# The values' projection moved between the recurrent group's convolutions and its gates

## The chip, the cores and the metric

The kernel runs on one core of a Trainium2 chip. The metric is the device time of one execution in microseconds (us). The kernel before has a median of 602.1 us in three runs (601.52 to 603.06).

The engines are called PE (matrix products), ACT (activations, casts), DVE (elementwise work and scans), POOL, and SP (here the queue that issues most transfers). Each works through its own list of instructions in order and waits where an input or a buffer is not ready.

## The reference

One decoder layer: 512 positions, 1024 features, all in float32.

```python
h = rms_norm(x, g_pre_mix)
q, k, v, xr, gr = split(h @ w_in)              # 512 columns each
attn = moba_attention(q, k, v, rel_bias)       # 8 heads of 64
xr = causal_dwconv(xr, w_conv_lru, b_conv_lru) # 4 taps per channel
r, i = sigmoid(xr @ w_r + b_r), sigmoid(xr @ w_i + b_i)  # block-diagonal
a = exp(-8 * r * softplus(-lam))
u = sqrt(1 - a * a) * (i * xr)
lru = scan(h_t = a_t * h_{t-1} + u_t) * gelu(gr)
x = x + rms_norm(concat(attn, lru) @ w_out, g_post_mix)
# then a convolved gated FFN (w_up, w_conv_ffn, w_down) in the same manner
```

## The kernel before

Every product of two float32 matrices is made of three matmuls on a high and a low part of each operand (`mm3`, lines 79 to 81: high*high, high*low, low*high). The split of an operand is a cast on ACT (`split`, line 84: `wh`, `xsh`, `mixTh`) and a subtraction on DVE (line 85: `wl`, `xsl`, `mixTl`). A weight block is loaded into a tile `raw` or `rawqk` (two buffers), split into `wh` and `wl` (four buffers each), and multiplied with `hTh`, `hTl`, the transposed normalized input.

The mixing stage, up to about 105 us, goes in this order in the source:

- `px`: the recurrent group's input (column `xr`), four blocks `t` of 128 channels, each 24 matmuls of 512 columns (the first two blocks in halves of 256). ACT starts each convolution with `xc` (line 309) and DVE adds three taps (line 311).
- Gates of block `t`, in the same loop: `xc` is split into `xsh`, `xsl` (one buffer each), six matmuls make `pg0` and `pg1` (line 317), and ACT and DVE make `a`, `g` and `y` of them (lines 321 to 332). The sigmoids are written with Tanh; Exp, Tanh, Abs and Square are used.
- `pv`: the values, four PSUM banks of 24 matmuls each (lines 335 to 344), split into `vhl` (line 356).
- `pgr`: the column `gr`, four blocks of 24 matmuls, each followed by a Gelu on ACT (line 362). Ahead of these in the source stands one Sqrt over all four blocks of `gv` (line 358).
- The scan: per block two multiplications (lines 364, 366) and one scan (line 365) on DVE, and the split of the result into `mixTh`, `mixTl` (line 367).
- `pq`: queries and keys of the first pair of heads, then attention pair by pair: scores `psc`, a softmax on DVE and ACT, transposes `ptp`, products `pav`. While a pair is in work, the next pair's `pq` matmuls are put between its steps.

The source order is not the order on the engines. The framework's scheduler fixes each engine's list when the program is built: it takes matmuls of one group between those of another, and moves casts and subtractions forward and back. An activation table load is put in front of an ACT function whose table isn't the active one.

Of the kernel before, what the change touches and what calls it, by code (L numbers as in the profile page):

```python
# [18 lines left out]
P = 128  # L19
# [5 lines left out]
DA = H * DH  # L25
DL = 512
NT = S // P
KD = D // P
# [24 lines left out]
def hybrid_layer(  # L53
# [8 lines left out]
    w_in, w_out, w_up, w_down = w_in[0], w_out[0], w_up[0], w_down[0]  # L62
# [7 lines left out]
    def bank(name, tag):  # L70
        return ps.tile([P, 512], F32, tag=tag, name=name, bufs=BANKS[tag])
# [5 lines left out]
    def mm3(o, lhs, rhs, start, stop):  # L77
        (lh, ll), (rh, rl) = lhs, rhs
        nc.tensor.matmul(o, lh, rh, start=start, stop=False)  # L79
        nc.tensor.matmul(o, lh, rl, start=False, stop=False)  # L80
        nc.tensor.matmul(o, ll, rh, start=False, stop=stop)  # L81

    def split(h, l, src, sub=None):
        nc.scalar.copy(h, src)  # L84
        (sub or nc.vector).tensor_sub(l, src, f32(h))  # L85

    def load_raw(src, k, n):
        t = wp.tile([P, k, n], F32, tag="raw", name="raw", bufs=2)
        nc.sync.dma_start(t, src.rearrange("(k p) n -> p k n", p=P))
        return t  # L90

    def split_w(src, k, n, sub=None):
        h = wp.tile([P, k, n], F32R, tag="wh", name="wh")
        l = wp.tile([P, k, n], F32R, tag="wl", name="wl")
        split(h, l, src, sub)
        return h, l

    def at(hl, *idx):
        return hl[0][idx], hl[1][idx]
# [57 lines left out]
    hT = [cp.tile([P, KD, S], F32R, tag=f"hT{i}", name=f"hT{i}") for i in "hl"]  # L157
# [61 lines left out]
    def w_conv_l(tap, t):  # L219
        return par[:, 4 * tap + t:4 * tap + t + 1]  # L220

    def col(c):
        return par[:, c:c + 1]
# [49 lines left out]
    def kpos(t):  # L273
        return sp[:, 6, t:t + 1]

    def kneg(t):
        return sp[:, 7, t:t + 1]
# [4 lines left out]
    def project(w, pt, c0=0, c1=S):  # L282
        for k in range(KD):
            mm3(pt[:, c0:c1], at(w, slice(None), k), at(hT, slice(None), k, slice(c0, c1)),
                k == 0, k == KD - 1)


    xc = lp.tile([P, NT, S], F32, name="xc")
    av = lp.tile([P, NT, S], F32, name="av")
# [3 lines left out]
    def xr_block(t):  # L293
        return split_w(raw_xr[t // 2][:, :, (t % 2) * P:(t % 2 + 1) * P], KD, P), bank("px", "mm")
# [5 lines left out]
    for t in range(NT):  # L300
        if t < 2:
            px = first[t][1]
        else:
            if t == 2:
                raw_xr.append(load_raw(w_in[:, XR0 + 256:XR0 + 512], KD, 256))
            w, px = xr_block(t)
            project(w, px)
        c = xc[:, t]
        nc.scalar.activation(c, px, AF.Identity, scale=w_conv_l(3, t), bias=col(16 + t))
        for d in range(1, 4):  # L310
            nc.vector.scalar_tensor_tensor(
                c[:, d:], px[:, :S - d], w_conv_l(3 - d, t), c[:, d:], op0=ALU.mult, op1=ALU.add)
        xs = [lp.tile([P, S], F32R, tag=f"xs{i}", name=f"xs{i}") for i in "hl"]
        split(xs[0], xs[1], c)
        pg = [bank(f"pg{g}", "sc") for g in range(2)]
        for g in range(2):
            mm3(pg[g], at(gw, slice(None), g, t), (xs[0], xs[1]), True, True)


        a, g, y = av[:, t], gv[:, t], gl[:, t]  # L320
        nc.vector.tensor_scalar(a, pg[0], col(20 + t), 0.0, op0=ALU.add, op1=ALU.min)
        nc.scalar.activation(g, pg[0], AF.Abs, scale=0.5, bias=half_b[:, t:t + 1])
        nc.scalar.activation(y, pg[1], AF.Tanh, scale=0.5, bias=half_b[:, 4 + t:5 + t])
        nc.vector.scalar_tensor_tensor(c, y, 1.0, c, op0=ALU.add, op1=ALU.mult)
        nc.scalar.activation(a, a, AF.Exp)
        nc.scalar.activation(g, g, AF.Tanh)
        nc.vector.scalar_tensor_tensor(g, g, 1.0, a, op0=ALU.add, op1=ALU.mult)

        nc.scalar.activation(a, g, AF.Exp, scale=kneg(t))
        nc.scalar.activation(g, g, AF.Tanh, scale=kpos(t))  # L330
        nc.scalar.activation(y, a, AF.Square)
        nc.vector.scalar_tensor_tensor(g, y, 1.0, g, op0=ALU.add, op1=ALU.mult)


    pv = [bank(f"pv{t}", ("tr", "tr", "av", "mm")[t]) for t in range(NT)]
    for c in range(2):
        raw = load_raw(w_in[c * 512:(c + 1) * 512, 2 * DA:3 * DA], 4, DA)
        for u in range(2):
            w = split_w(raw[:, 2 * u:2 * u + 2], 2, DA)
            for j in range(2):  # L340
                k = 4 * c + 2 * u + j
                for t in range(NT):
                    mm3(pv[t], at(hT, slice(None), k, slice(t * P, (t + 1) * P)),
                        at(w, slice(None), j), k == 0, k == KD - 1)

    def gr_block(t):
        if t % 2 == 0:
# [246 lines left out]
    for i2 in range(NF // 2):  # L594
        raws = [load_raw(w_up[:, o + 256 * i2:o + 256 * (i2 + 1)], KD, 256) for o in (0, DFF)]
        blocks = [[], []]
        for b in range(2):
            for r in raws:
                w = split_w(r[:, :, b * P:(b + 1) * P], KD, P, None if i2 else nc.gpsimd)
# [55 lines left out]
```

## Time and profile before

| | |
|---|---|
| median of 3 runs | 602.1 us |
| the profiled execution's own time | 601.9 us |
| its span in the trace | 600.1 us |
| PE busy | 581.0 us (97% of the span), 2704 matmuls |
| DVE busy | 364.0 us (61%) |
| ACT busy | 277.6 us (46%) |
| granted PE clock, mean | 0.993 |

The span runs from the first to the last instruction of the profiled execution; 1.8 us of its time lie outside. Busy matmuls overlap, since one starts before the one ahead of it has ended: the pace is the distance of their starts, not their duration. A start-to-start distance is used for ACT and DVE as well where instructions follow each other without a wait.

### The profile page before, as it was taken

The page shows a single profiled execution, that of the slowest core. Times are in us where ns is not written, and L with a number is a line of the kernel's source. Part 1 is how long each engine was busy: PE and PEld are TensorE (multiplying, and loading weights), DVE is VectorE, ACT ScalarE, POOL GpSimd, SP SyncE. Part 2 cuts the span into 40 slices and gives each one's busy share as a digit, 9 for nine tenths or more (in the row PEclk, how much of TensorE's full clock was granted, in tenths as well). Part 3 has the DMA queues.
Part 4 walks back from the last instruction along what each step waited for, and adds up shares of the span by engine and source line. Part 5 has one row for each costly group of instructions (what it writes and reads, how often), then busy time and mean ns, then how long its engine had stood idle before and what let it go on. Part 6 is the DMA issues. An engine that isn't in the chain of part 4 may idle for free.

```text
span 600.1 us, 6975 instructions
## 1 busy us (share of the span) xinstructions
PE 581.0 (97%) x2704; PEld 475.9 (79%) x2704; DVE 364.0 (61%) x660; ACT 277.6 (46%) x455; POOL 11.6 (2%) x12
## 2 busy tenths in 40 slices
PE   6999999999999997999999999999999999999995
PEld 3977888677778876988888888888888888888884
DVE  5869694788885688476566566665665622232225
ACT  7539954667765463454344443443444412231221
POOL 1000000000000033000000000000000000000000
PEclk9999999999999998999999999999999999999998
DMA  7552445233020405044034124224314421332103
GB/s 229 188 211 72 139 117 163 72 106 97 9 71 1 140 2 175 1 141 141 13 128 140 52 90 141 70 71 140 97 44 141 134 77 37 140 114 97 35 1 140
DMA packets 52265, 59.62 MB, mean 99 GB/s; under 512 B 2448, under 2 KB 41568, under 8 KB 52233
## 3 DMA queue, kind: packets, MB, share of 16 engines
q1 hardware_dynamic: 51201, 57.61, 29.8%
q10 hardware_dynamic: 1032, 1.57, 0.8%
q8 instruction: 21, 0.34, 0.2%
q14 instruction: 11, 0.09, 0.0%
HBM read 57.06 MB, written 3.69 MB: 101 GB/s over the span
## 4 chain that ended last, share of the span: by engine, by line
PE 92%; DVE 4%; ACT 2%; DMA 1%; issue 0%; SPq 0%; DVEq 0%
PE pup L80 13%; PE pup L79 13%; PE pup L81 13%; PE py L79 9%; PE py L80 9%; PE py L81 9%; PE pq L79 3%; PE pq L80 2%; PE pq L81 2%; PE psc L425 2%; PE pav L451 2%; PE ptp L441 2%; PE px L81 1%; PE px L79 1%; PE px L80 1%; PE pv L79 1%
## 5 line engine op out<-in xcount | busy, mean ns | idle before, releaser
L85 DVE TENSOR_TENSOR wl<-raw,wh 128x1024 fp32r<-128x1024 f32 x82 | 100.2, 1222 | 133.9 <-ACT wh L84 133.2
L84 ACT CAST wh<-raw 128x1024 fp32r<-128x1024 f32 x86 | 89.9, 1048 | 156.0 <-PE py L81 72.0
L80 PE MATMUL pup<-h2Tl,wh 128*128 128x512 f32 (+1 forms) x384 | 143.4, 373 | 2.0 <-DVE h2Tl L85 2.0
L81 PE MATMUL pup<-h2Th,wl 128*128 128x512 f32 (+1 forms) x384 | 143.5, 374 | 0.0
L79 PE MATMUL pup<-h2Th,wh 128*128 128x512 f32 (+1 forms) x384 | 143.3, 373 | 0.0
L80 PEld LDWEIGHTS pup<-h2Tl,wh 128*128 128x128 f32 x384 | 73.1, 190 | 14.5 <-DVE h2Tl L85 2.3
L79 PEld LDWEIGHTS pup<-h2Th,wh 128*128 128x128 f32 x384 | 73.1, 190 | 12.6
L81 PEld LDWEIGHTS pup<-h2Th,wl 128*128 128x128 f32 x384 | 73.0, 190 | 12.5
L79 PE MATMUL py<-wh,acth 128*128 128x512 f32 x176 | 68.5, 389 | 0.0
L80 PE MATMUL py<-wl,acth 128*128 128x512 f32 x176 | 68.5, 389 | 0.0
L81 PE MATMUL py<-wh,actl 128*128 128x512 f32 x176 | 68.5, 389 | 0.0
L81 PEld LDWEIGHTS py<-wh,actl 128*128 128x128 f32 x176 | 33.0, 188 | 6.9
L80 PEld LDWEIGHTS py<-wl,acth 128*128 128x128 f32 x176 | 33.0, 188 | 6.8
L79 PEld LDWEIGHTS py<-wh,acth 128*128 128x128 f32 x176 | 33.0, 188 | 6.8
L589 ACT ACTIVATE yg<-yg 128x512 f32<-128x512 f32 x22 | 13.9, 633 | 42.7 <-DVE yg L582 42.7
L582 DVE SCALAR_TENSOR_TENSOR yu<-pup,par,yu 128x511 f32<-128x511 f32 (+1 forms) x44 | 33.0, 749 | 0.8
L582 DVE SCALAR_TENSOR_TENSOR yg<-pup,par,yg 128x511 f32<-128x511 f32 (+1 forms) x44 | 32.8, 746 | 0.8
L79 PE MATMUL pq<-hTh,wh 128*128 128x512 f32 x64 | 26.5, 414 | 0.0
L80 PE MATMUL py<-wl,mixTh 128*128 128x512 f32 x64 | 25.8, 404 | 0.0
L81 PE MATMUL py<-wh,mixTl 128*128 128x512 f32 x64 | 25.5, 399 | 0.0
L81 PE MATMUL pq<-hTh,wl 128*128 128x512 f32 x64 | 25.5, 399 | 0.0
L79 PE MATMUL py<-wh,mixTh 128*128 128x512 f32 x64 | 25.4, 397 | 0.0
(164 smaller groups left out, 849.0 us busy)
## 6 DMA issues: line engine op xcount, KB each, us to landing
raw<-in_w_up_dram SPq DMA_DIRECT2D x22, 1024.0 KB, 5.2
raw<-in_w_down_dram SPq DMA_DIRECT2D x10, 1024.0 KB, 5.0
raw<-in_w_in_dram SPq DMA_DIRECT2D x5, 1024.0 KB
rawqk<-in_w_in_dram SPq DMA_DIRECT2D x8, 512.0 KB, 5.2
raw<-in_w_out_dram SPq DMA_DIRECT2D x4, 1024.0 KB, 5.1
xres<-in_x_dram SPq DMA_DIRECT2D x4, 512.0 KB, 6.0
out_dram<-yz SPq DMA_DIRECT2D x8, 256.0 KB, 2.0
toep<-fbd ACTq DMA_DIRECT2D x1, 1536.0 KB
```

What stands on the lines that cost most here:

```text
L79: nc.tensor.matmul(o, lh, rh, start=start, stop=False)
L80: nc.tensor.matmul(o, lh, rl, start=False, stop=False)
L81: nc.tensor.matmul(o, ll, rh, start=False, stop=stop)
L84: nc.scalar.copy(h, src)
L85: (sub or nc.vector).tensor_sub(l, src, f32(h))
L425: nc.tensor.matmul(psc[:, :W], qs[own[s], s, qi], kl[own[s], :W], start=False, stop=True)
L441: nc.tensor.transpose(ptr[:, j * P:(j + 1) * P], st[:, j * P:(j + 1) * P], ident)
L451: nc.tensor.matmul(pav[:, j * P:], vs, pT[i][:, j * S:j * (S - P) + S], start=j == 0 and i == 0, stop=j == NT - 1 and i == 1)
L582: nc.vector.scalar_tensor_tensor(y[:, d:], pt[:, :S - d], w_conv_f(2 - d, blk), y[:, d:], op0=ALU.mult, op1=ALU.add)
L589: nc.scalar.activation(yg, yg, AF.Gelu_apprx_tanh)
```

## The change

The loop over `t` is cut in two. The first loop keeps the projections `px` and the convolutions. Then come the values (`pv`), and after them a second loop with the split of `xc`, the gate products and the gate functions. No instruction of the computation is added or taken away.

```diff
         for d in range(1, 4):
             nc.vector.scalar_tensor_tensor(
                 c[:, d:], px[:, :S - d], w_conv_l(3 - d, t), c[:, d:], op0=ALU.mult, op1=ALU.add)
-        xs = [lp.tile([P, S], F32R, tag=f"xs{i}", name=f"xs{i}") for i in "hl"]
-        split(xs[0], xs[1], c)
-        pg = [bank(f"pg{g}", "sc") for g in range(2)]
...
-        nc.vector.scalar_tensor_tensor(g, y, 1.0, g, op0=ALU.add, op1=ALU.mult)
     pv = [bank(f"pv{t}", ("tr", "tr", "av", "mm")[t]) for t in range(NT)]
...
                 for t in range(NT):
                     mm3(pv[t], at(hT, slice(None), k, slice(t * P, (t + 1) * P)),
                         at(w, slice(None), j), k == 0, k == KD - 1)
+
+
+    for t in range(NT):
+        c = xc[:, t]
+        xs = [lp.tile([P, S], F32R, tag=f"xs{i}", name=f"xs{i}") for i in "hl"]
+        split(xs[0], xs[1], c)
+        pg = [bank(f"pg{g}", "sc") for g in range(2)]
+        for g in range(2):
+            mm3(pg[g], at(gw, slice(None), g, t), (xs[0], xs[1]), True, True)
+
+
+        a, g, y = av[:, t], gv[:, t], gl[:, t]
+        nc.vector.tensor_scalar(a, pg[0], col(20 + t), 0.0, op0=ALU.add, op1=ALU.min)
+        nc.scalar.activation(g, pg[0], AF.Abs, scale=0.5, bias=half_b[:, t:t + 1])
+        nc.scalar.activation(y, pg[1], AF.Tanh, scale=0.5, bias=half_b[:, 4 + t:5 + t])
+        nc.vector.scalar_tensor_tensor(c, y, 1.0, c, op0=ALU.add, op1=ALU.mult)
+        nc.scalar.activation(a, a, AF.Exp)
+        nc.scalar.activation(g, g, AF.Tanh)
+        nc.vector.scalar_tensor_tensor(g, g, 1.0, a, op0=ALU.add, op1=ALU.mult)
+
+        nc.scalar.activation(a, g, AF.Exp, scale=kneg(t))
+        nc.scalar.activation(g, g, AF.Tanh, scale=kpos(t))
+        nc.scalar.activation(y, a, AF.Square)
+        nc.vector.scalar_tensor_tensor(g, y, 1.0, g, op0=ALU.add, op1=ALU.mult)
```

Lines from the gates on have other numbers in the change: the gate lines 321 to 332 become 337 to 348, the Sqrt 358 becomes 362, the Gelu 362 becomes 366, the scan lines 364 to 366 become 368 to 370, `vhl` 356 becomes 360. The lists of the two programs differ on the engines at three places that matter below. A number behind a name tells buffers apart; `wh_842` and `wh_846` belong to the first pair's queries and keys (`pq_850`, `pq_875`), `wl_920` to the second pair's queries (`pq_937`).

On PE, around 41 us of the trace before, where the fourth block of `px` begins (`px_506` before, `px_437` in the change). Before:

```order
L79 MATMUL pv1_559<-wh_592,hTh_82 128x512
L79 MATMUL pv2_560<-wh_592,hTh_82 128x512
L79 MATMUL px_506<-hTh_82,wh_502 128x512
L79 MATMUL pg0_398<-xsh_394,gwh_108 128x512
L79 MATMUL pg1_399<-xsh_394,gwh_108 128x512
L80 MATMUL px_506<-hTl_83,wh_502 128x512
```

In the change:

```order
L79 MATMUL pv1_467<-wh_500,hTh_82 128x512
L79 MATMUL pv2_468<-wh_500,hTh_82 128x512
L79 MATMUL px_437<-hTh_82,wh_433 128x512
L80 MATMUL px_437<-hTl_83,wh_433 128x512
L81 MATMUL px_437<-hTh_82,wl_434 128x512
```

The gate products of the first block no longer stand behind the first matmul of `px`. They now stand 99 matmuls later, behind the last matmul of `pv`; those of the blocks 1 to 3 follow 20, 41 and 76 matmuls behind the first ones, between the `pgr` matmuls.

On ACT, from the end of the gates to the first `pgr` Gelu. Before:

```order
L356 CAST vhl_93<-pv0_558 128x4x2x64
L358 ACT_TABLE_LOAD
L358 ACTIVATE gv_282<-gv_282 128x2048
L84 CAST wh_694<-raw_688 128x1024
L356 CAST vhl_93<-pv1_559 128x4x2x64
L356 CAST vhl_93<-pv2_560 128x4x2x64
L356 CAST vhl_93<-pv3_561 128x4x2x64
L84 CAST wh_842<-rawqk_839 128x1024
L362 ACT_TABLE_LOAD
L362 ACTIVATE gl_283<-pgr_707 128x512
```

In the change, the piece from the third Gelu to the fourth:

```order
L366 ACT_TABLE_LOAD
L366 ACTIVATE gl_283<-pgr_759 128x512
L345 ACT_TABLE_LOAD
L345 ACTIVATE av_281<-gv_282,sp_253 128x512
L84 CAST wh_842<-rawqk_839 128x1024
L346 ACTIVATE gv_282<-gv_282,sp_253 128x512
L347 ACTIVATE gl_283<-av_281 128x512
L84 CAST wh_846<-rawqk_839 128x1024
L362 ACT_TABLE_LOAD
L362 ACTIVATE gv_282<-gv_282 128x2048
L366 ACT_TABLE_LOAD
L366 ACTIVATE gl_283<-pgr_785 128x512
```

The first three Gelus stand among the gates of blocks 1 to 3, each with a table load ahead of it and another behind it. From the first gate function to the last Gelu ACT has eight table loads where it had two. The cast `wh_842`, which stood ahead of the first Gelu, now stands behind the third and behind the Exp of the last block, and the Sqrt stands behind `wh_846`.

On DVE, from the split of the keys' weights `wl_847` to the split of the second pair's weights. Before:

```order
L365 SCALAR_TENSOR_TENSOR gv_282<-av_281,xc_280 128x512 x2
L85 TENSOR_TENSOR mixTl_89<-gl_283,mixTh_88 128x512
L85 TENSOR_TENSOR wl_843<-rawqk_839,wh_842 128x1024
L85 TENSOR_TENSOR wl_847<-rawqk_839,wh_846 128x1024
L366 TENSOR_TENSOR gl_283<-gl_283,gv_282 128x512
L85 TENSOR_TENSOR mixTl_89<-gl_283,mixTh_88 128x512
L85 TENSOR_TENSOR wl_920<-rawqk_916,wh_919 128x1024
```

In the change:

```order
L85 TENSOR_TENSOR wl_847<-rawqk_839,wh_846 128x1024
L368 TENSOR_TENSOR xc_280<-xc_280,gv_282 128x512 x2
L369 SCALAR_TENSOR_TENSOR gv_282<-av_281,xc_280 128x512 x2
L370 TENSOR_TENSOR gl_283<-gl_283,gv_282 128x512 x2
L368 TENSOR_TENSOR xc_280<-xc_280,gv_282 128x512 x2
L85 TENSOR_TENSOR mixTl_89<-gl_283,mixTh_88 128x512 x2
L369 SCALAR_TENSOR_TENSOR gv_282<-av_281,xc_280 128x512 x2
L370 TENSOR_TENSOR gl_283<-gl_283,gv_282 128x512 x2
L85 TENSOR_TENSOR wl_920<-rawqk_916,wh_919 128x1024
```

All four scans (line 365, now 369) stood ahead of `wl_843` before; in the change they stand, with their multiplications, between `wl_847` and `wl_920`.

## Rows read from the trace of the kernel before

**Rows 1.** The page's part on the chain of work that ended last: shares of the span by engine.

```profile
PE 92%; DVE 4%; ACT 2%; DMA 1%; issue 0%; SPq 0%; DVEq 0%
```

**Rows 2.** PE's waits over the whole span: tile and line that waited, what it waited for, us in total, times, longest us.

```profile
PE ptr L151 <- DVE hn L145: 4.8, 3, 3.0
PE pup L80 <- DVE h2Tl L85: 2.0, 1, 2.0
PE pg L79 <- issue: 1.5, 1, 1.5
```

**Rows 3.** PE's timeline at the fourth `px` block: start us, duration us, engine, line, operation, in brackets the idle time before it.

```profile
41.05 0.39 PE L79 MATMUL px<-hTh,wh 128*128 128x512 f32 x1
42.90 0.70 PE L79 MATMUL pg<-xsh,gwh 128*128 128x512 f32 x2 [1.46 <-issue]
```

**Rows 4.** ACT's timeline at the same place.

```profile
41.23 1.04 ACT L84 CAST wh<-raw 128x1024 fp32r<-128x1024 f32 x1 [3.04 <-DMA raw<-in_w_in_dram]
42.19 0.61 ACT L84 CAST xsh<-xc 128x512 fp32r<-128x512 f32 x1
```

**Rows 5.** PE's timeline: the first `pgr` matmul, the first and the third of the first pair's `pq` (96 and 98 matmuls later), and the third of the second pair's (48 later again).

```profile
71.13 0.39 PE L79 MATMUL pgr<-hTh,wh 128*128 128x512 f32 x1
...
92.89 0.39 PE L79 MATMUL pq<-hTh,wh 128*128 128x512 f32 x1
...
93.34 0.39 PE L81 MATMUL pq<-hTh,wl 128*128 128x512 f32 x1
...
104.22 0.39 PE L81 MATMUL pq<-hTh,wl 128*128 128x512 f32 x1
```

**Rows 6.** ACT's timeline, a stretch of gate functions that follow each other without a wait.

```profile
48.91 0.69 ACT L323 ACTIVATE gl<-pg,half_b 128x512 f32<-128x512 f32 x1 [1.06 <-PE pg L81]
49.49 0.71 ACT L329 ACTIVATE av<-gv,sp 128x512 f32<-128x512 f32 x1
50.11 0.68 ACT L322 ACTIVATE gv<-pg,half_b 128x512 f32<-128x512 f32 x1
50.67 0.72 ACT L330 ACTIVATE gv<-gv,sp 128x512 f32<-128x512 f32 x1
51.29 0.62 ACT L331 ACTIVATE gl<-av 128x512 f32<-128x512 f32 x1
51.81 0.62 ACT L325 ACTIVATE av<-av 128x512 f32<-128x512 f32 x1
52.33 0.62 ACT L326 ACTIVATE gv<-gv 128x512 f32<-128x512 f32 x1
52.85 0.61 ACT L84 CAST xsh<-xc 128x512 fp32r<-128x512 f32 x1
53.36 0.79 ACT L309 ACTIVATE xc<-px,par 128x512 f32<-128x512 f32 x1
```

**Rows 7.** ACT's timeline: the Sqrt and the first Gelu with their table loads, and the cast `wh_842` between.

```profile
69.89 1.28 ACT L358 ACT_TABLE_LOAD   x1
71.19 1.92 ACT L358 ACTIVATE gv<-gv 128x2048 f32<-128x2048 f32 x1
...
76.54 1.05 ACT L84 CAST wh<-rawqk 128x1024 fp32r<-128x1024 f32 x1 [1.05 <-PE pgr L80]
77.62 1.28 ACT L362 ACT_TABLE_LOAD   x1
78.91 0.60 ACT L362 ACTIVATE gl<-pgr 128x512 f32<-128x512 f32 x1
```

**Rows 8.** DVE's timeline: two scans, two multiplications, one multiplication, and the splits `wl_843` and `wl_847`.

```profile
77.28 2.33 DVE L365 TENSOR_TENSOR_SCAN gv<-av,xc 128x512 f32<-128x512 f32 x2
79.53 1.27 DVE L364 TENSOR_TENSOR xc<-xc,gv 128x512 f32<-128x512 f32 x2
80.71 0.69 DVE L366 TENSOR_TENSOR gl<-gl,gv 128x512 f32<-128x512 f32 x1
...
84.15 2.36 DVE L85 TENSOR_TENSOR wl<-rawqk,wh 128x1024 fp32r<-128x1024 f32 x2
```

**Rows 9.** Stretches of the span: from:to, length, busy us (instructions) of PE, PEld, DVE, ACT, POOL, then the granted PE clock (1.00 is 2.4 GHz, 0.50 is 1.2 GHz), DMA share, GB/s.

```profile
42.00:43.00 1.00, 0.10 (x1) 0.13 (x2) 0.17 (x1) 0.80 (x2) 0.00 (x0) 1.00 0.43 159
...
226.00:227.00 1.00, 0.82 (x6) 0.82 (x7) 1.00 (x3) 0.00 (x0) 1.00 (x1) 0.91 0.00 0
227.00:228.00 1.00, 1.00 (x7) 1.00 (x7) 1.00 (x1) 0.00 (x0) 0.76 (x1) 0.50 0.00 0
...
230.00:231.00 1.00, 1.00 (x9) 1.00 (x9) 0.91 (x4) 1.00 (x4) 0.00 (x0) 0.88 1.09 388
...
235.00:236.00 1.00, 0.98 (x9) 1.00 (x10) 1.00 (x2) 0.32 (x1) 0.00 (x0) 1.00 0.85 241
...
595.50:596.00 0.50, 0.00 (x0) 0.00 (x0) 0.46 (x2) 0.00 (x0) 0.00 (x0) 0.50 0.00 0
```

**Rows 10.** PE's timeline: matmuls of 256 columns at either level of the clock.

```profile
227.56 0.41 PE L79 MATMUL pup<-h2Th,wh 128*128 128x256 f32 x1
227.78 0.41 PE L80 MATMUL pup<-h2Tl,wh 128*128 128x256 f32 x1
...
230.42 0.28 PE L81 MATMUL pup<-h2Th,wl 128*128 128x256 f32 x1
230.54 0.28 PE L79 MATMUL pup<-h2Th,wh 128*128 128x256 f32 x1
```

More of the change, by code (lines that the diff above doesn't have):

```diff
@@ L312, in hybrid_layer @@
                 c[:, d:], px[:, :S - d], w_conv_l(3 - d, t), c[:, d:], op0=ALU.mult, op1=ALU.add)
+    pv = [bank(f"pv{t}", ("tr", "tr", "av", "mm")[t]) for t in range(NT)]
+    for c in range(2):
+        raw = load_raw(w_in[c * 512:(c + 1) * 512, 2 * DA:3 * DA], 4, DA)
+        for u in range(2):
+            w = split_w(raw[:, 2 * u:2 * u + 2], 2, DA)
+            for j in range(2):
+                k = 4 * c + 2 * u + j
+                for t in range(NT):
+                    mm3(pv[t], at(hT, slice(None), k, slice(t * P, (t + 1) * P)),
+                        at(w, slice(None), j), k == 0, k == KD - 1)
+    for t in range(NT):
+        c = xc[:, t]
         xs = [lp.tile([P, S], F32R, tag=f"xs{i}", name=f"xs{i}") for i in "hl"]
@@ L332, in hybrid_layer @@
         nc.vector.scalar_tensor_tensor(g, y, 1.0, g, op0=ALU.add, op1=ALU.mult)
[L335 to L344, printed above, removed]
     def gr_block(t):
```

## The prediction

> **What bounds the kernel now.** I read the chain of work that ended last first: 92% of it is PE [rows 1]. So a change is worth what it adds to or takes from PE's waits, and the next view is the list of these. Up to the end of attention it has one wait at the place of the change: 1.5 us at `pg` [rows 2]. PE's timeline there shows the first `px` matmul of the fourth block at 41.05 and the next matmul, the first gate product, at 42.90 [rows 3]. ACT's timeline says why: the cast `xsh`, which the gate product reads, starts only at 42.19, behind a weight cast that waited 3.04 us for its load until 41.23 [rows 4]. That load is the second half of the values' weights, which PE doesn't need yet.
>
> From there PE runs without a listed wait into attention. Its pace is (92.89 - 71.13) / 96 = 0.2267 us per matmul of 512 columns [rows 5]. ACT and DVE have slack in this stretch, but they feed PE from short lists of buffers, so the question is when ACT and DVE reach the splits for `pq`.
>
> **What the change saves.** The first gate products leave their place behind `px`. PE goes on at 41.05 + 0.23 = 41.28 instead of 42.90: 1.62 us saved. What covers the late load now is the rest of `px` and the values' matmuls on the first half of their weights: 51 matmuls x 0.2267 = 11.6 us, up to 52.6, while the cast of the late half ends at 42.3. Without that cover the 1.62 us would come back. The number of matmuls is the same, so their work costs nothing more.
>
> **What it moves, first term: `pq` waits for its weights.** The gate functions now start after the values. The last `pv` matmul starts 98 places behind 41.05, at 63.3, and ends at 63.7. ACT has one weight cast ahead of the rest, whose buffer is only free then (1.04, by [rows 4]), and a cast of `vhl`, which I take like a gate cast at 0.52. The first Tanh starts near 65.2, when its product is also done. From here ACT's list is summed with the distances of starts in [rows 6]: Tanh of the gate 0.58, Abs 0.56, both Exp 0.52 and 0.62, the other Tanhs 0.52 and 0.62, Square 0.52, cast `xsh` 0.51 (0.61 where something waits for its end). A table load takes 1.30 up to the next function, a Gelu 0.60 [rows 7].
>
> - Block 0: 0.58 + 0.56 + 0.52 + 0.52 + 0.51 = 2.69, up to 67.9. Then a wait of 0.6 for DVE, which has a `wl`, a `vhl` and two gate pieces ahead of the one that is needed (1.13 and three to four at 0.6 by [rows 8], from 64.8). Then 0.72 + 0.62 + 0.52, up to 70.4.
> - Block 1: the five pieces to the end of `xsh` without Abs, 0.58 + 0.52 + 0.52 + 0.61, and Abs 0.56: 2.8. Load, Gelu, load: 3.2. Exp, the next block's Abs, Tanh, Square: 2.32. Up to 78.7.
> - Block 2: the same without the first Abs, 2.23 + 3.2 + 2.32, up to 86.5.
> - Block 3: 0.58 + 0.52 + 0.62, load, Gelu, load 3.2, Exp 0.62, up to 92.0; then `wh_842`, 1.05, up to 93.1.
>
> PE, with 219 matmuls behind 41.05 and some 0.6 us lost at the gate products (0.4 of it a wait for `xsl` of block 1, behind the same DVE pieces), would be at `pq` at 91.3. It waits for `wh_842` till 93.1, and for the third matmul, which reads `wl_843`, until 93.1 + 1.23 [rows 8] = 94.4. Before, that matmul started at 93.34 [rows 5]. So the saving is gone here and PE is 1.1 us late. In the kernel before the same cast ran at 76.54 [rows 7], 16 us ahead of its use: the cover is used up by six more table loads (7.8 us) and by gates that start 20 us later.
>
> The Trainium skill, page "ScalarE: Activation LUTs", section "What ACT_TABLE_LOAD costs", puts a switch at about 2.66 us: 1.28 for the load and 1.38 for a drain. The trace agrees with the first part (1.28) and shows no room for the second: the load at 77.62 follows a cast that ends at 77.59, and the Gelu starts 0.01 behind the load [rows 7]. By the page's figure as an estimate, six more switches would put another 6 x 1.38 = 8.3 us into ACT's sum and the whole near 618.
>
> **Second term: the second pair's weights wait behind the scan.** After `wh_842` ACT has Tanh, Square and `wh_846` (up to 95.2), a load (96.5) and the Sqrt, 1.92 [rows 7], up to 98.4. Only then can DVE start the first multiplication of the recurrence. Its list up to `wl_920` is five pairs at 1.2 (a pair starts 80.71 - 79.53 = 1.18 ahead of the next piece), two pairs of scans at 2.25, and the split itself at 1.23 [rows 8]: 6.0 + 4.5 + 1.2 = 11.7, up to 110.1, and 110.2 with the handovers. The Gelu of the last block (97.7) and the casts of `mixTh` on ACT lie beside this. PE would be at the third matmul of `pq_937`, which reads `wl_920`, 48 x 0.2267 = 10.9 us behind 94.4, at 105.3. It waits 4.9 us there. Nothing else is queued on PE that could go ahead: it takes its matmuls in order. Before, that matmul started at 104.22 [rows 5], so PE is now 6.0 us late. This includes the 1.62 saved and the 1.1 above; it is not added to them.
>
> **Third term: the clock.** A PE that sits idle for 4.9 us may lose its clock. Rows of both kinds exist. After the 1.96 us idle at `pup` (2.0 in [rows 2]) the granted clock was 0.91 in the microsecond from 226 and 0.50 in the next, and 0.88 in that from 230 [rows 9]: some 3.3 us at 1.2 GHz. After the 3.0 us at `ptr` it stayed at 1.00 in the microsecond from 235, as it did after the 1.5 us at 42 [rows 2, 9]. At the end of the program, where no matmul follows, it was 0.50 from 595.5. At the lower level 256 columns took 0.22 against 0.12 [rows 10]; 15 of them fit into 3.3 us, and 15 x 0.095 = 1.4 us is the price. Bounds: 0 and, for two such stretches, 2.8. I take 1.4, since this idle time is longer than any of the three above. A fall during the wait at `pq_850` costs nothing: PE waits for DVE behind it anyway.
>
> **Sum.** 601.9 (the profiled execution) + 6.0 + 1.4 = 609.3. The median of the runs is 0.2 above the profiled one, so 609.5. Nothing after `pq_937` is counted. DVE comes to the first softmax some 2.3 us later in relation to PE than before, which the slower matmuls just then would cover; if they don't, 1 to 2 us more are lost, and this goes into the range. The queue of SP keeps its order up to the bias tables `tb`, which now stand ahead of the last pair's weights; the tables wait for the last `mixTl`, near 111.6, and are read by the first softmax near 116, some 4 us, so I count no wait there.
>
> **Rivals.** (a) *The saving alone.* If ACT and DVE reach `wh_842` and `wl_920` in time after all, only the 1.62 us are left: 602.1 - 1.6 = 600.5. For it speaks the 16 us that `wh_842` had in hand before [rows 7]; against it the sums above, which would have to be wrong by 2 us at the first and by 5 us at the second place. It decides from the point where `wh_842` ends before 91.3 and `wl_920` before 102.2. (b) *Only the first wait.* If DVE's scans overlap better than the rows say, PE is late by 1.1 us: 603.2. Two scans at 2.25 in a row speak against it. (c) *Attention loses too.* The clock falls, and the later softmaxes hold PE up by 2 to 3 us more: 612. DVE's slack there is small. (d) *The heavier switch.* If a switch of tables held ACT as long as two loads, 6 x 1.3 = 7.8 more would reach `wl_920`: 617. The two switches in [rows 7], with no gap on either side of the load, speak against it. The page named above would have it so.
>
> **How the numbers follow.** The forecast (both waits, with or without the clock's fall) 0.74, and of this 0.5 with the fall; its own range is 607.0 to 611.5. (a) 0.06, (b) 0.06, (c) 0.10, (d) 0.04. A measurement of this kernel can tell about 0.3%, 1.8 us, from no change. Half of (a) is faster than that, the other half and (b) are within it, the rest is slower: 0.03, 0.09, 0.88. The range from 606.0 to 612.6 leaves out (a), (b), (d) and the upper end of (c). It takes in an error of about 2 us in ACT's and DVE's sums and the clock's bounds from 0 up.
>
> **What would show it.** Right: no wait at 41 us; eight table loads on ACT from 65 to 98 us; PE's wait at `pq` of some 2 + 0.8 us near 92 for ACT and DVE; a second one of 4 to 5 us that ends near 110 with `wl` on DVE, the last of the work from the Sqrt through the scans; a granted clock of 0.50 for about 3 us right behind it. Wrong: a `pq` that starts at 91.3 without a wait; a Sqrt before 95; or later waits in attention larger than these two together.

## The result and the profile after

The changed kernel takes 609.94 us (median of four runs, 608.88 to 610.34) against 602.15 us for the kernel before in the same rounds: ratio 1.0121, 95% interval 1.0106 to 1.0135. The forecast was 609.5. The profiled execution took 610.34 us, with a span of 608.5 and a mean granted clock of 0.988.

The chain of work that ended last shows ACT and DVE with 6% each, where they had 2% and 4% [rows 1]:

```profile
PE 86%; ACT 6%; DVE 6%; DMA 1%; issue 0%; SPq 0%; DVEq 0%
```

PE's waits over the whole span (tile and line, what it waited for, us in total, times, longest us) answer to [rows 2]. The wait at `pg` is gone, two at `pq` are new, and the longest at `ptr` has grown from 3.0 to 4.5:

```profile
PE ptr L151 <- DVE hn L145: 5.9, 2, 4.5
PE pq L81 <- DVE wl L85: 5.1, 2, 4.6
...
PE pup L80 <- DVE h2Tl L85: 2.0, 1, 2.0
PE pq L79 <- ACT wh L84: 1.7, 1, 1.7
```

PE's timeline: first the fourth `px` block, against [rows 3]; then the end of `pgr`, the first and third matmul of the first pair's `pq`, and the second pair's, against [rows 5]. In brackets is the idle time before the matmul.

```profile
40.88 0.39 PE L79 MATMUL px<-hTh,wh 128*128 128x512 f32 x1
41.11 0.39 PE L80 MATMUL px<-hTl,wh 128*128 128x512 f32 x1
...
90.59 0.39 PE L81 MATMUL pgr<-hTh,wl 128*128 128x512 f32 x1
92.70 0.50 PE L79 MATMUL pq<-hTh,wh 128*128 128x512 f32 x1 [1.72 <-ACT wh L84]
...
93.96 0.50 PE L81 MATMUL pq<-hTh,wl 128*128 128x512 f32 x1 [0.53 <-DVE wl L85]
...
104.77 0.39 PE L80 MATMUL pq<-hTl,wh 128*128 128x512 f32 x1
109.75 0.80 PE L81 MATMUL pq<-hTh,wl 128*128 128x512 f32 x1 [4.60 <-DVE wl L85]
110.34 0.63 PE L79 MATMUL pq<-hTh,wh 128*128 128x512 f32 x1
110.77 0.63 PE L80 MATMUL pq<-hTl,wh 128*128 128x512 f32 x1
```

ACT's timeline, against [rows 7]: the first gate function, one Gelu between its two table loads, and the end of the gates. The cast at 91.62 is `wh_842`.

```profile
64.95 0.69 ACT L339 ACTIVATE gl<-pg,half_b 128x512 f32<-128x512 f32 x1
...
72.74 1.28 ACT L366 ACT_TABLE_LOAD   x1
74.03 0.60 ACT L366 ACTIVATE gl<-pgr 128x512 f32<-128x512 f32 x1
74.65 1.28 ACT L345 ACT_TABLE_LOAD   x1
...
91.62 1.03 ACT L84 CAST wh<-rawqk 128x1024 fp32r<-128x1024 f32 x1
...
94.75 1.28 ACT L362 ACT_TABLE_LOAD   x1
96.04 1.92 ACT L362 ACTIVATE gv<-gv 128x2048 f32<-128x2048 f32 x1
97.98 1.28 ACT L366 ACT_TABLE_LOAD   x1
```

DVE's timeline behind the Sqrt, against [rows 8]. The last row is `wl_920`:

```profile
97.99 1.29 DVE L368 TENSOR_TENSOR xc<-xc,gv 128x512 f32<-128x512 f32 x2 [2.00 <-ACT gv L362]
99.20 2.33 DVE L369 TENSOR_TENSOR_SCAN gv<-av,xc 128x512 f32<-128x512 f32 x2
101.45 1.26 DVE L370 TENSOR_TENSOR gl<-gl,gv 128x512 f32<-128x512 f32 x2
102.64 1.28 DVE L368 TENSOR_TENSOR xc<-xc,gv 128x512 f32<-128x512 f32 x2
103.84 1.28 DVE L85 TENSOR_TENSOR mixTl<-gl,mixTh 128x512 fp32r<-128x512 f32 x2
105.05 2.33 DVE L369 TENSOR_TENSOR_SCAN gv<-av,xc 128x512 f32<-128x512 f32 x2
107.30 1.27 DVE L370 TENSOR_TENSOR gl<-gl,gv 128x512 f32<-128x512 f32 x2
108.48 1.22 DVE L85 TENSOR_TENSOR wl<-rawqk,wh 128x1024 fp32r<-128x1024 f32 x1
```

DVE works without a gap from the end of the Sqrt to `wl_920`, and PE's matmul at 109.75 starts just behind it.

The clock around that wait and at the start of the feed-forward part (from:to, length, busy us and instructions of PE, PEld, DVE, ACT, POOL, granted PE clock, DMA share, GB/s), against [rows 9]:

```profile
108.00:110.00 2.00, 0.25 (x1) 0.25 (x2) 2.00 (x3) 1.21 (x2) 0.00 (x0) 0.91 0.00 0
110.00:112.00 2.00, 2.00 (x5) 1.59 (x6) 2.00 (x3) 1.06 (x2) 0.00 (x0) 0.50 0.00 0
112.00:114.00 2.00, 2.00 (x8) 1.57 (x7) 1.94 (x4) 1.65 (x3) 0.00 (x0) 0.73 0.71 179
114.00:116.00 2.00, 2.00 (x11) 1.45 (x10) 1.94 (x3) 0.67 (x2) 0.00 (x0) 1.00 1.08 186
...
234.00:236.00 2.00, 2.00 (x19) 2.00 (x18) 1.21 (x1) 0.76 (x1) 0.66 (x1) 1.00 0.09 25
...
242.00:244.00 2.00, 2.00 (x10) 2.00 (x11) 1.44 (x3) 0.70 (x2) 0.00 (x0) 0.50 0.92 310
244.00:246.00 2.00, 2.00 (x12) 2.00 (x11) 1.37 (x4) 1.82 (x4) 0.00 (x0) 0.50 0.60 198
246.00:248.00 2.00, 2.00 (x17) 2.00 (x17) 1.70 (x4) 0.00 (x0) 0.00 (x0) 0.95 0.00 0
```

To see where the 8.4 us of span come from, I use three places on PE that every kernel has: the fourth `px` block, the matmul of `pup` (the up-projection) that waits at the start of the feed-forward part, and the `ptr` (a transpose on PE) that waits 8.8 us later. In the kernel before the last two are

```profile
226.18 0.38 PE L80 MATMUL pup<-h2Tl,wh 128*128 128x256 f32 x1 [1.96 <-DVE h2Tl L85]
235.02 1.06 PE L151 MATMUL ptr<-ident,hn 128*128 128x128 f32 x8 [3.00 <-DVE hn L145]
```

and in the kernel after

```profile
233.07 0.39 PE L80 MATMUL pup<-h2Tl,wh 128*128 128x256 f32 x1 [1.97 <-DVE h2Tl L85]
241.91 1.94 PE L151 MATMUL ptr<-ident,hn 128*128 128x128 f32 x8 [4.52 <-DVE hn L145]
```

From `px` to `pup` is 226.18 - 41.05 = 185.13 before and 233.07 - 40.88 = 192.19 after: **7.06 us more**. This distance leaves out what differs between two executions up to 41 us (the fourth `px` block starts at 39.8 to 41.1 in the kernels below) and what happens behind `pup`; it serves for all experiments. At the `pq` of the second pair it was (109.75 - 40.88) - (104.22 - 41.05) = 5.70 more; from there to `pup` another 1.36 comes in. At `ptr` the two are still 6.89 apart on the span's own scale, and at the end 8.4: **1.5 us come in behind `ptr`**. I put them down to the clock. From `pup` to `ptr` it is 8.84 us in both kernels, so DVE sets this distance, not PE. Before, the clock fell within it [rows 9], and the time that PE lost came out of its wait, which was 3.00. After, it stayed at 1.00 there (the row from 234) and PE waited 4.52; the clock fell in that wait and was still at 0.50 for some 4 us of matmuls behind it, where no wait was left to hide them. The nine profiles of this document bear this out. From this `ptr` to the end it is 365.1 us in the three where the clock is at 1.00 behind it (before, experiments 2 and 3), and 365.9 to 367.4 in the six where it is at 0.50 there, least with under 3 us at 0.50 (experiment 6) and most with 6 (experiment 5). Whether the change moves this fall or the execution does isn't shown by one profile of each: the four runs of the change have a mean granted clock of 0.988 to 0.990, those of the kernel before in the experiments' rounds 0.986 to 0.996.

Together: 601.9 - 0.17 (the earlier `px`) + 5.70 + 1.36 + 1.5 = 610.3, the time of the profiled execution.

### The profile page after: what moved, and what is told of

The parts are those of the page before. It is cut to its first block, busy times and chain, and to the rows that moved or that the text cites. A ratio compares the mean times of both kernels' runs of the same rounds, so it can differ in the third digit from the quotient of the medians.

```text
span 608.5 us, 6988 instructions
## 1 busy us (share of the span) xinstructions
PE 582.3 (96%) x2704; PEld 476.4 (78%) x2704; DVE 363.4 (60%) x660; ACT 286.2 (47%) x461; POOL 11.6 (2%) x12
## 4 chain that ended last, share of the span: by engine, by line
PE 86%; ACT 6%; DVE 6%; DMA 1%; issue 0%; SPq 0%; DVEq 0%
PE pup L81 13%; PE pup L80 13%; PE pup L79 13%; PE py L80 9%; PE py L79 9%; PE py L81 9%; PE pq L79 2%; PE pq L81 2%; PE pq L80 2%; PE psc L429 2%; PE pav L455 2%; PE ptp L445 2%; PE px L81 1%; PE px L79 1%; PE px L80 1%; PE pv L81 1%
## 5 line engine op out<-in xcount | busy, mean ns | idle before, releaser
L80 PE MATMUL pq<-hTl,wh 128*128 128x512 f32 x64 | 26.0, 406 | 0.0
```

## Experiments

### 1. The Gelus behind all gates

The six extra table loads are the first suspect, so this run takes them away. Each Gelu is queued on ACT behind the Sqrt, and the `pgr` products get two more banks, so that PE need not wait for the Gelus.

```diff
-    nc.scalar.activation(gv, gv, AF.Sqrt, scale=0.25)
+    root_gv = nc.scalar.activation(gv, gv, AF.Sqrt, scale=0.25)
     for t in range(NT):
-        pg = bank("pgr", "mm")
+        pg = bank("pgr", ("mm", "mm", "tr", "tr")[t])
         project(w_gr[t], pg)
-        nc.scalar.activation(gl[:, t], pg, AF.Gelu_apprx_tanh)
+        with tc.issue_after(root_gv.ins):
+            nc.scalar.activation(gl[:, t], pg, AF.Gelu_apprx_tanh)
```

> The changed kernel, but the four Gelus are queued on ACT behind the Sqrt, so that no table is switched among the gates (three loads from the first gate function to attention's first Exp instead of eight behind the gates), and the last two pgr blocks get other PSUM banks so that PE needs no early Gelu. My theory (six table loads and the Gelus between them make the gates late, and with them the first pair's weights and the recurrence): ACT is through its gates some 9.6 us earlier, near 83, both waits at pq vanish, and only the saved 1.6 us are left: 600.5 us, up to 602 if the clock falls in another place at the feed-forward part's start. Rival (the gates behind the values are too late by themselves, tables or not): a wait at pq stays, 604 us or more.

Measured: 607.48 us (604.4 to 607.83); ratio to before 1.0068, interval 1.0041 to 1.0095. Both waits at `pq` are gone, as the theory had it, but the time did not come down to 602: the rival had the time (604 or more), though not the place. PE's timeline shows a new wait at attention's first scores:

```profile
106.77 0.47 PE L429 MATMUL psc<-sk,sq 128*128 128x128 f32 x2 [1.87 <-DVE sq L417]
...
110.60 0.69 PE L429 MATMUL psc<-sk,sq 128*128 128x384 f32 x1 [0.36 <-DVE sm L433]
```

and the clock behind it:

```profile
106.00:108.00 2.00, 1.23 (x5) 0.91 (x5) 1.94 (x3) 1.66 (x4) 0.00 (x0) 0.82 0.96 253
108.00:110.00 2.00, 2.00 (x5) 1.16 (x4) 0.06 (x1) 1.83 (x2) 0.00 (x0) 0.50 1.06 218
...
116.00:118.00 2.00, 2.00 (x6) 1.08 (x5) 0.77 (x3) 0.00 (x0) 0.00 (x0) 0.62 0.00 0
```

On DVE `sq`, the split of the first pair's queries, starts at 105.94, directly behind the recurrence and three splits of weights. The second wait, 0.36, is another matter: DVE's first softmax stood idle 2.19 us until 110.25 for the bias tables `tb`. From `px` to `pup` (230.87) this kernel takes 189.96 us, 4.83 more than before. The waits account for -1.62 + 1.87 + 0.36 = 0.6 of it; the other 4.2 go with the clock, which is at half from 107 to 117 us, and at the end another 1.1 comes in behind `ptr`. So the table loads, with the Gelus among the gates, were the cause of the `pq` waits, but not of the whole loss: the recurrence without them is still late, for the next one who needs DVE.

### 2 and 3. Each scan twice, in the change and before

Here the length of the recurrence is changed and nothing else, once in each order. Both kernels get one more scan per block, with the same inputs and output:

```diff
         nc.vector.tensor_tensor_scan(gv[:, t], av[:, t], xc[:, t], 0.0, op0=ALU.mult, op1=ALU.add)
+        nc.vector.tensor_tensor_scan(gv[:, t], av[:, t], xc[:, t], 0.0, op0=ALU.mult, op1=ALU.add)
```

In the change:

> The changed kernel with each of the four scans done twice on DVE (the second writes the same values). My theory (the second wait hangs on DVE's list from the Sqrt through the scans to wl_920): four more scans of 1.12 us stand ahead of that split and one multiplication of 0.6 goes behind it, so 3.9 us more: 613.8 us, and a second wait of 8.5 us instead of 4.6. Rival (the second wait hangs on ACT's casts or on PE's banks, and DVE's scans lie beside them): no change, 609.9 us.

In the kernel before:

> The same doubled scans in the kernel before, as a control. My theory: there the recurrence starts at 73 us and the weights for pq are needed at 93 us and later, so 4.5 us more on DVE are hidden: 602.1 us, no change, and no wait at pq. Rival (DVE is a bound of this stage in either order): 604 to 606.6 us.

Measured: in the change 613.61 us (612.6 to 615.02; ratio to before 1.0183, interval 1.0163 to 1.0203), 3.7 more than without the doubling. PE's second wait grew to

```profile
112.52 0.79 PE L81 MATMUL pq<-hTh,wl 128*128 128x512 f32 x1 [8.45 <-DVE wl L85]
```

that is, by 3.85 us. In the kernel before: 602.14 us (ratio 0.999, interval 0.9975 to 1.0005), with no wait at `pq`. The same 4.5 us of DVE work cost nothing in the old order and nearly their whole length in the new one: the recurrence now lies on the path that sets the end, and before it didn't.

That the median rose by nearly the forecast 3.9 is in part chance. In the profiled execution the clock was at 0.50 for 5.8 us behind the longer wait, and from `pq` to `pup` (236.90) it took 1.06 us more than in the change; against that, the 1.5 us behind `ptr` were not there.

```profile
116.00:118.00 2.00, 2.00 (x6) 1.52 (x6) 1.94 (x4) 1.66 (x4) 0.00 (x0) 0.50 0.88 264
```

### 4. The second pair's split ahead of half of the recurrence

If only `wl_920` is the matter, it can go ahead. The weights of the first two pairs are loaded and split earlier in the source, and blocks 2 and 3 of the recurrence are queued behind `wl` of the second pair.

```diff
+    w_qk = {0: qk_weights(0)}
+    for t in range(2):
+        recur(t)
+    w_qk[1] = qk_weights(1)
+    with tc.issue_after(subs[-1].ins):
+        for t in range(2, NT):
+            recur(t)
```

> The changed kernel with the second pair's weights loaded and split ahead of the blocks 2 and 3 of the recurrence, by an edge of order on DVE. My theory (the whole recurrence is late, and wl_920 is only the first thing behind it): the wait at wl_920 vanishes, since that split ends at 103.9, but PE then waits some 5 us at the first scores, because the attention's tiles lie where the recurrence's tiles lay and wait for its last split, near 113; 608.7 us, 1.2 us less than the changed kernel. Rival (the place of wl_920 in DVE's list is the cause): the wait of 4.6 us and the clock's fall go, 604 us.

Measured: 613.07 us (612.07 to 613.85; ratio 1.0171, interval 1.0154 to 1.0188), slower than the change itself. The wait at `wl_920` is gone; in its place PE waits twice for attention's first tile:

```profile
114.50 0.77 PE L447 MATMUL psc<-sk,sq 128*128 128x128 f32 x2 [5.05 <-DVE sq L435]
...
116.66 0.76 PE L79 MATMUL pq<-hTh,wh 128*128 128x512 f32 x1 [0.67 <-DVE sq L435]
```

ACT's part of that tile, the cast, started behind the recurrence's last `mixTl`, as expected:

```profile
112.54 0.58 ACT L434 CAST sq<-pq 64x512 fp32r<-64x512 f32 x1 [0.77 <-DVE mixTl L85]
```

DVE's part started at 113.67, behind one more split of weights (1.2 us), so not all of the 5.05 is the recurrence's own length.

The rival (the split alone is late, 604 us) falls: with this split ahead of half of the recurrence, the next consumer waits. The loss was larger than I expected for the same wait moved to another place. The clock goes with that:

```profile
114.00:116.00 2.00, 1.49 (x4) 1.00 (x4) 1.91 (x4) 1.94 (x5) 0.00 (x0) 0.50 0.94 205
...
124.00:126.00 2.00, 2.00 (x6) 1.36 (x6) 0.49 (x3) 0.00 (x0) 0.00 (x0) 0.55 0.00 0
```

From `px` (40.20) to `pup` (236.58) it takes 11.25 us more than before. The first wait makes PE 0.8 late and the two waits above are 5.7; some 4.7 remain, while the clock is at half from the end of the wait to nearly 126. The change itself lost 1.4 in this way.

### 5. The wait filled with matmuls that nobody reads

What part of the loss is the clock's alone? In the change 18 matmuls on data that is already there write to a free bank; the scheduler put 4 of them into the first wait and 14 into the second.

```diff
+        if pr == 1:
+            idle = bank("idle", "av")
+            for n in range(18):
+                nc.tensor.matmul(idle, ws_first[0][0][:, n % KD], hT[0][:, n % KD],
+                                 start=True, stop=True)
+        ws_first[:] = ws
```

> The changed kernel with 18 matmuls of 512 columns that nothing reads put on PE ahead of pq_937: four of them fall into the first wait, 14 into the second (3.2 us). My theory (the second wait of 4.6 us costs another 1.4 us because the granted clock is at 1.2 GHz for some 3 us behind it): PE idles for only about 1 us at wl_920, the clock stays at 1.00 there, and pq_937's first split still arrives at 109.7: 608.5 us, 1.4 us less in spite of 18 matmuls more. Rival (the fall of the clock is covered by DVE's and ACT's lateness in attention): no change, 609.9 us. Second rival (the added matmuls delay PE): up to 610.3 us.

Measured: 610.25 us (607.04 to 610.45, six runs; ratio 1.0117, interval 1.0096 to 1.0138), no gain over the change. At the place itself it did what was meant: the matmul that waits for `wl_920` starts at the same time as in the change, 68.87 us behind its `px` block, after a shorter idle time, and the clock stays up:

```profile
109.78 0.50 PE L81 MATMUL pq<-hTh,wl 128*128 128x512 f32 x1 [1.35 <-DVE wl L85]
...
110.00:112.00 2.00, 2.00 (x10) 1.61 (x10) 2.00 (x3) 1.23 (x3) 0.00 (x0) 1.00 0.00 0
```

At `pup` (232.12 - 40.91 = 191.21) it is 0.98 ahead of the change. So the half-speed stretch at 110 us was worth 1.0 us of the 1.36 between `pq` and `pup`. Then the feed-forward part took it back: the clock was at 0.50 from 234 to 236, which cost nothing up to `ptr`, and again from 241 to 247, and behind `ptr` this kernel took 0.8 us more than the change. The second rival (the added matmuls delay PE) has the time, 610.3, but not the cause, since at `wl_920` and at `pup` PE was no later than in the change. The mean granted clock was 0.996 in the two shortest of the six runs (607.04 and 607.47), and 0.989 in the others. What the clock does at the start of the feed-forward part differs between executions of one kernel, and I did not find out what decides it.

### 6. The saving alone

The kernel before, with only the wait at 41 us removed: the casts and splits of the late half of the values' weights are queued behind the first block's `xsh`. The gates stay where they were.

```diff
+        if t == 0:
+            xsh0 = casts[-1]
...
-            w = split_w(raw[:, 2 * u:2 * u + 2], 2, DA)
+            if c:
+                with tc.issue_after(xsh0.ins):
+                    w = split_w(raw[:, 2 * u:2 * u + 2], 2, DA)
+            else:
+                w = split_w(raw[:, 2 * u:2 * u + 2], 2, DA)
```

> The kernel before with one edge of order on ACT: the weight cast that waits for the late load is queued behind the cast xsh of the first gate block. My theory (the 1.62 us that the change saves at 41 us is only that order on ACT): the wait at 41 us goes and nothing else moves: 600.5 us. Rival (the gap comes from somewhere else, or is given back at the next gate block): 602.1 us.

Measured: 600.19 us (598.83 to 601.17, seven runs; ratio 0.9968, interval 0.9954 to 0.9981). This is the fastest of all kernels here. `px` to `pup` (223.55 - 40.15 = 183.40) is 1.73 us shorter than before, for the 1.62 of the prediction. The time agrees with the forecast 600.5 in part by chance: this execution came to `px` 0.9 us earlier than the one before, and lost 0.8 behind `ptr`, where the clock was at 0.50. The saving was real; up to `pup` the change paid 7.06 + 1.62 = 8.7 us for it.

### 7. The recurrence left out

If the second wait is the recurrence and nothing else, it must go when the recurrence goes, with gates, Gelus and table loads left where the change puts them.

```diff
     for t in range(NT):
-        nc.vector.tensor_mul(xc[:, t], xc[:, t], gv[:, t])
-        nc.vector.tensor_tensor_scan(gv[:, t], av[:, t], xc[:, t], 0.0, op0=ALU.mult, op1=ALU.add)
         nc.vector.tensor_mul(gl[:, t], gl[:, t], gv[:, t])
```

> The change, with the recurrence's first multiplication and its scan left out on all four blocks (8 DVE instructions of the 12 between the Sqrt and the split of the second pair's weights; the output is therefore another one). Gates, Gelus, table loads and the Sqrt stay where the change puts them. Theory: the second wait is made of the recurrence's own length on DVE and nothing else. Then the Sqrt still ends near 98, the last Gelu near 99.9, four casts of mixTh and the cast of the second pair's queries end near 103, their split on DVE near 104.3, before PE wants it at 105.0: no wait there, no half-speed stretch behind it, and only the first wait is left (third matmul of the first pair's queries at 93.96 against 93.34, 0.6 us late): 602.1 + 0.6 = 602.7 us; with the later fall of the clock at the start of the feed-forward part that the change showed, up to 604.2. Rival: gates, Sqrt and table loads that end 26 us later than before hold attention's first tiles up by themselves, so PE waits 1.5 to 5 us at the first scores as in the two runs that moved the recurrence's order: 605 to 609 us.

Measured: 603.73 us (602.83 to 605.71, ten runs; ratio 1.0019, interval 1.0002 to 1.0037). The first wait is there unchanged, and nothing is left of the second:

```profile
92.91 0.50 PE L79 MATMUL pq<-hTh,wh 128*128 128x512 f32 x1 [1.72 <-ACT wh L84]
...
94.17 0.50 PE L81 MATMUL pq<-hTh,wl 128*128 128x512 f32 x1 [0.53 <-DVE wl L85]
...
105.20 0.39 PE L81 MATMUL pq<-hTh,wl 128*128 128x512 f32 x1
...
226.83 0.38 PE L80 MATMUL pup<-h2Tl,wh 128*128 128x256 f32 x1 [1.97 <-DVE h2Tl L85]
```

The matmul at 105.20 reads the second pair's split without a wait, and the clock doesn't fall there. `px` (41.05) to `pup` is 185.78, 0.65 more than before, where 0.62 was expected. Behind `ptr` this profile again has the clock at 0.50 (234 to 240) and loses (602.3 - 600.1) - (235.68 - 235.02) = 1.5 us. Together that is 2.2 in this execution; the median of ten stands 1.7 above the kernel before (602.0 in the same rounds). The rival (gates and table loads hold attention up by themselves) falls.

## Why the prediction was right, step by step

**The saving, 1.62.** Right. PE's matmuls at 40.88 and 41.11 follow each other at full pace, and experiment 6 measures 1.73.

**First term.** Right in place, cause and size. The first gate Tanh started at 64.95 (forecast 65.2), the gates reached `wh_842` 0.4 us sooner (its end is at 92.65, forecast 93.1), and PE waited 1.72 + 0.53 us for ACT and DVE. The third matmul came at 93.96 for a forecast 94.4; from `px` on that makes PE 0.8 us late where 1.1 was expected. The error is in ACT's sum: it began 0.25 earlier, and its wait for DVE ahead of block 0's Exp was 0.25 for 0.6. The 0.6 us that were to be lost at the gate products were 0.3: the last `pgr` matmul started at 90.59, so PE was ready for `pq` at 90.8. Experiment 1 shows the cause: without the loads and Gelus among the gates both waits are gone.

**The table switch.** Each of the eight loads takes 1.28 us, starts at most 0.03 behind the end of the instruction ahead of it, and the next function starts 0.01 to 0.02 behind it: 72.74, 74.03, 74.65 above. The Trainium skill, page "ScalarE: Activation LUTs", section "What ACT_TABLE_LOAD costs", adds a drain of about 1.38 us to each switch. None of the eight switches here shows it, and the time near 618 that this would have given did not come. Rival (d) is out with it.

**Second term.** Right in place and cause, 0.3 too large. The Sqrt ended at 97.96 (forecast 98.4). DVE's list to `wl_920` took 109.7 - 98.0 = 11.7, as summed. The wait was 4.60 for 4.9, and PE 5.7 us late for 6.0. Experiments 2, 3 and 7 show the cause by its length: 3.85 us more wait for 4.5 us more scans, no cost in the old order, and no wait without the recurrence.

**The clock.** The fall was predicted behind the wait, at 1.4 us, and stands there: 0.50 from 110 to 112, 0.73 to 114, with matmuls of 512 columns at 0.43 against 0.2267 us. From `pq` to `pup` 1.36 us come in; experiment 5 shows 1.0 of them to be the clock's. So the price of 1.4 was 0.4 too high.

**Attention at nothing.** Right within the 0.4 us that then remain, whose cause is open; they make good the 0.4 of the clock. Rival (c) did not come about. Rivals (a) and (b) are out by the waits.

**What was not in the sum.** The 1.5 us behind `ptr`. I had read the fall of the clock at 227 [rows 9] only as a price list, and not asked what it cost there (nothing, since PE waited 3.00 us at `ptr` all the same) and whether the change would move it. Two other parts stand against it: the 0.3 of the second term, and the 0.2 by which this execution came to `px` earlier. The forecast's median also had 0.2 added to the profiled time, while this median is 0.4 below it. So the forecast is 0.4 from the median although one part of 1.5 was missing: the mechanism up to `pup` was right, but this closeness is luck.

Experiments 1 and 4 correct one more reading. I had put the six table loads first among the reasons for the late gates, and expected both waits and the loss to go with them. They are part of it, but without them the recurrence is still late by 2 us at the next consumer, and a short wait there cost more through the clock than through itself.

## What to carry to other kernels

A load that is waited for at one place and a chain of small functions that feeds DVE are two different covers: before moving the chain to cover the load, sum what stands behind the chain on each in-order engine, up to the first operand that the busiest engine needs from it. Here it was cheaper to reorder the one cast that stood in the way (experiment 6) than to move the work. When a wait is shortened or moved, look at the granted clock behind it, since the clock can cost nearly two times the wait (experiment 1: 4.2 us behind 2.2).

## What the runs showed of the hardware that was not expected

**A short wait can cost more than a long one.** Behind the 4.60 us wait in the change the clock was back at 1.00 within 4 us. Behind the 8.45 us of experiment 2 it stayed at half for some 6 us, behind the 1.87 us of experiment 1 for some 10, and behind the 5.05 us of experiment 4 for some 11. In experiments 1 and 4 the matmuls of scores stand among those of 512 columns, but that alone doesn't explain it: in experiment 2 only matmuls of 512 columns ran in those 6 us, thirteen of them, and in experiment 1 ten of them in a row, from 111.83 to 115.84, without the clock coming back. What decides it stays open.

**The same idle time doesn't always lower the clock.** At `pup` PE idles 1.96 to 1.97 us before, after and in experiment 7; behind it the clock fell before (0.50 at 227) and stayed at 1.00 in the other two. At `ptr` it stayed up through 3.00 us before and 3.01 in experiment 2, and fell in 4.52 in the change, but also in 3.03 in experiment 5 and 3.02 in experiment 6. Per execution this is worth 1 to 2 us, as much as the saving that the change was made for, and it stays open what decides it.
